# First stage of a hybrid decoder kernel: latents leave PSUM on ScalarE, norm reciprocals in token columns, weights split two chunks ahead, a gate chunk moved

## The chip, the cores and the metric

The kernel runs on one core of a Trainium2 chip. The metric is the device time of one launch in microseconds (us), the median of three runs. The engines are called as in the profile: PE (TensorE; PEld is its weight load), DVE (VectorE), ACT (ScalarE), POOL (GpSimd) and SP (SyncE, which here only issues DMAs).

## The reference, cut to what matters

A decoder trunk over 2048 tokens of width 1024: two branches on one normed input, recurrence (RWKV-7) and latent attention, merged by gates, then a mixture of experts. The change is in the first part alone, which projects the input and prepares both branches:

```python
h = rmsnorm(x, mix_norm_g[l])
cols = h @ w_in[l]
c_rw  = cols[..., :RW_COLS]                       # recurrence: r, k, v and three small inputs
c_q   = cols[..., RW_COLS:RW_COLS + Q_LORA]       # 384 query latents
c_kv  = cols[..., ...:... + KV_LORA]              # 256 key-value latents
c_kr  = cols[..., ...:RW_COLS + MLA_COLS]         # 32 rotary key columns
gate_rw  = jax.nn.sigmoid(cols[..., ...])         # 1024
gate_mla = jax.nn.sigmoid(cols[..., ...])         # 1024
y_rw  = rwkv7_mix(c_rw, ...)
# in mla_mix:
q  = (rmsnorm(q_d,  g_qa)  @ w_q_up)
kv = (rmsnorm(kv_d, g_kva) @ w_kv_up)

def rmsnorm(x, g):
    y = x * lax.rsqrt(jnp.mean(x * x, axis=-1, keepdims=True) + NORM_EPS)
    return y * g
```

## The kernel before

Everything is held transposed, columns of the projection in partitions and tokens along the free axis. `phase_a` goes through two halves of 1024 tokens, each as two blocks (n = 0, 1) of 512. The projection's columns are cut into chunks of 128. For one chunk and one block `a_mm` runs 24 products 128x128x512 (`mm3`: weights and input are each split into a high and a low part in the fast f32 format, and three of the four products are kept), into one of the four PSUM banks tagged `am`. All other products of the stage use four banks tagged `rw`.

Weights: `a_weights` loads a chunk (512 KB) into one of two `awr` buffers. `a_split` makes the two parts of it, `aw0` and `aw1`, two buffers each: a copy on ACT (L143), then a subtraction (L144), on DVE for the first part of a half and on POOL for the later one. `a_mm` keeps two chunks split (`len(self.live) < 2`). `worder` is the order of the chunks: 14 of the recurrence, five gate chunks, two of key-value latents, three of query latents, one gate chunk, the rotary key, ten gate chunks.

The input's norm is not applied to the input. `x_squares` adds squares of the raw input (ACT, then POOL), and `x_rms` turns the sums over partitions into `xrs`, the factor of each token, repeated over all 128 partitions: one product with a matrix of ones (`sums`, L214), a square root on ACT, a reciprocal on DVE, both over 128x512. Each evicted block is multiplied by `xrs` on its way out of PSUM: `cols` for the recurrence, `gate` (L633, then a tanh on ACT and a store), and `mla_evac` (L259) for the latents, which also squares them (ACT, L261) and adds the squares up in `zacc` (DVE, L263). Latents wait in `zc`, two buffers. `mla_norm` then makes a second factor `zrs` for the latents in the same way with `sums`, multiplies and splits them (L283); `mla_up` multiplies them with the up-projections.

The recurrence units (`rw_unit`, eight in each half) prepare each pair of heads: decays, keys, `f` (the factor on the key and then the key itself, L521 and L522), the masked score products `aa` (L551, L554), and at the end three transposes that go through the tile `tok` (L592, one buffer) to DRAM by four stores each.

`invert` is a triangular inverse on DVE, 124 small operations that run behind everything else from the key-value chunks to the end of the half.

Generators in a list (`gens`) are advanced by `bg(k)` after each block; the order in which the program writes instructions is a priority. What each engine really executes, and in which order, is planned when the kernel is built: a list scheduler with a timeline simulation takes, on each engine, the ready instruction with the highest priority, and hands out the buffers. The result is a fixed order for each engine, and the engine waits wherever the chip is later than the plan.

Of the kernel before, what the change touches and what calls it, by code (L numbers as in the profile page):

```python
# [44 lines left out]
BIG = 1 << 20  # L45

CST = {}
CFIRST = 128


def _consts():
# [36 lines left out]
class K:  # L88
# [67 lines left out]
    def rope_tables(self, pool):  # L156
# [3 lines left out]
        self.ropeT = self.dram("ropeT", [2, 8, 16, S])  # L160
        pi = pool.tile(sh, I32, name="posi")
        self.dma(pi, self.I["pos"])
        a, n, z, s, c, u = (pool.tile(sh, F32, name="rt_" + k) for k in "anzscu")
        nc.gpsimd.tensor_copy(u, pi)
        nc.gpsimd.tensor_scalar(a, u, self.c["invp"], None, op0=OP.mult)
        ts = lambda o, i, s1, s2, o1, o2: nc.gpsimd.tensor_scalar(o, i, s1, s2, op0=o1, op1=o2)
# [40 lines left out]
            self.dma(xs[:, k], self.I["xT"][k, :, c0:c0 + 512])  # L207
        return xs

    def sums(self, acc, n, scale):  # L210

        nc = self.nc
        ps = self.pst("rw", 4)
        nc.tensor.matmul(ps, self.c["ones"], acc, start=True, stop=True)  # L214
        nc.scalar.activation(n, ps, AF.Sqrt, scale=scale, bias=self.eps[:, 0:1])
        nc.vector.reciprocal(n, n)

    def x_squares(self, pool, xs, n):
        nc = self.nc
# [6 lines left out]
            yield  # L226

    def x_rms(self, n):
        self.rs[n] = self.ap.tile([128, 512], F32, name="xrs%d" % n)
        self.sums(self.xacc[n], self.rs[n], 1.0 / D)  # L230

    def h_make(self, xs, n, k):

# [19 lines left out]
    def mla_evac(self, pool, ps, key, n, j):  # L253
        nc = self.nc
        if j == 0:
            self.zc[key, n] = (pool.tile([128, 3, 512], F32, name="zc", bufs=2),
                               pool.tile([128, 512], F32, name="zacc", bufs=2))
        zc, acc = self.zc[key, n]
        nc.vector.tensor_tensor(out=zc[:, j], in0=ps, in1=self.rs[n], op=OP.mult)  # L259
        sq = pool.tile([128, 512], F32, name="zsq") if j else acc  # L260
        nc.scalar.activation(sq, zc[:, j], AF.Square)  # L261
        if j:
            nc.vector.tensor_tensor(out=acc, in0=acc, in1=sq, op=OP.add)  # L263
# [9 lines left out]
    def mla_norm(self, pool, key, n):  # L273
        nc = self.nc
        zc, acc = self.zc.pop((key, n))
        nk, g0, dim = (3, 50, 384) if key == "q" else (2, 53, 256)
        yield "w"
        yield "w"
        rt = pool.tile([128, 512], F32, name="zrs")
        self.sums(acc, rt, 1.0 / dim)  # L280
        cT = [pool.tile([128, 3, 512], F32R, name="cT%d" % j, bufs=2) for j in range(2)]
        for k in range(nk):
            nc.vector.scalar_tensor_tensor(zc[:, k], zc[:, k], self.pv[:, g0 + k:g0 + k + 1], rt,  # L283
                                           op0=OP.mult, op1=OP.mult)
            self.split(cT[0][:, k], cT[1][:, k], zc[:, k])
        self.cT[n] = cT
# [136 lines left out]

    def a_split(self):
        rv = self.wraw.pop(0)
        hl = [self.ap.tile([128, 8, 128], F32R, name="aw%d" % j, bufs=2) for j in range(2)]
        if rv.shape[2] == 64:

            hl = [hl[0][:, :, :64], hl[0][:, :, 64:], hl[0]]
        self.split(hl[0], hl[1], rv, self.nc.gpsimd if self.wsplit > 1 and self.wsplit % 35 > 18 else None)  # L430
        self.live.append((self.worder[self.wsplit], hl))
        self.wsplit += 1
        self.a_weights()

    def a_mm(self, ci, n, last):
        while len(self.live) < 2 and self.wraw:
            self.a_split()
        w = dict(self.live)[ci]
        ht = self.ht[n]
# [23 lines left out]
    def rw_unit(self, pool, p, q, zr, zk, zv, x1, xg):  # L463
# [117 lines left out]
        for j, src in enumerate(("b", "k", "v")):  # L581
# [6 lines left out]
            ps = self.pst("rw", 4)  # L588
            for i in range(4):
                nc.tensor.transpose(ps[:, i * 128:(i + 1) * 128], x[:, i * 128:(i + 1) * 128], self.ident)  # L590
            tk = t("tok")
            A.activation(tk, ps, AF.Copy)  # L592
            tv = tk.rearrange("p (c h d) -> p c h d", c=4, h=2)
            for e in range(2):
# [5 lines left out]
    def phase_a(self):  # L600
# [3 lines left out]
        with ExitStack() as st:  # L604
# [2 lines left out]
            ap = self.ap = st.enter_context(pool("acols"))  # L607
            self.rw_setup()
            self.mla_setup()
            self.worder = 2 * (tuple(range(14)) + G[:5] + KV + Q + G[5:6] + ("kr",) + G[6:])  # L610
            self.wpos = self.wsplit = 0
            self.wraw, self.live, self.ht, self.zc, self.rs, self.cT, self.xacc = [], [], [[None] * 8, [None] * 8], {}, {}, {}, {}
            gens = []

            def bg(k):
# [42 lines left out]
            xp = start.enter_context(pool("start"))  # L658
            self.consts()
            xs = [self.x_load(xp, 0, 0, True)]  # L660
            self.dma(self.c["ones"], self.I["cst"][:, :CFIRST])
            xs.append(self.x_load(xp, 0, 1))
            for n in range(2):
                gens.append(self.x_squares(xp, xs[n], n))
# [4 lines left out]
            for half in range(2):  # L669
# [46 lines left out]
                with pool("mla%d" % half) as mp:  # L716
# [7 lines left out]
                            bg(3)  # L724
                    next(inv)
                    gens.append(self.mla_up(mp, "kv", half))
                    for j, ci in enumerate(Q):
                        for n in range(2):
                            self.mla_evac(mp, self.a_mm(ci, n, n == 1), "q", n, j)
                            if j == 2:  # L730
                                gens.append(self.mla_norm(mp, "q", n))
                            bg(3)
                            next(inv, None)
                    gens.append(self.mla_up(mp, "q", half))
                    for ci in G[5:6] + ("kr",) + G[6:6]:
                        for n in range(2):
                            if ci == "kr":
                                self.kr_evac(mp, self.a_mm("kr", n, n == 1), half * 1024 + n * 512, n)
                            else:
                                gate(ci, n, half)  # L740
                            bg(3)
                            next(inv, None)
                    drain()
                with pool("gates%d" % half) as gp:
                    if half == 0:
# [1066 lines left out]
```

## Time and profile before

| | us |
|---|---|
| three runs | 2708.5, 2710.17, 2712.07 |
| median | 2710.17 |
| profiled execution | 2706.18 |
| its span, first to last instruction | 2704.4 |

The profiled execution is one more run, with the hardware profiler on. Its trace tells for each instruction when it ran, how long the engine was idle before it, and which semaphore ended that wait. A busy share is a mean over stages; what a change in a stage is worth is read from the waits in that stage. The granted clock is the share of TensorE's full clock that the chip allows at a time.

### The profile page before, as it was taken

What the parts mean: (1) busy time and instruction counts of PE and PEld (TensorE: products, weight loads), DVE (VectorE), ACT (ScalarE), POOL (GpSimd) and SP (SyncE); (2) the same over time, 40 slices, a digit from 0 to 9 for tenths busy, and PEclk for the clock granted to TensorE, in tenths of its full rate; (3) what the DMA queues carried; (4) which work ended last, traced back from release to release, by engine and by line L of the source; (5) the groups of instructions that cost most, each with busy time, mean ns of one, the idle gap of its engine ahead of it and who ended that gap; (6) DMA issues with size and microseconds to landing.
All of it is one profiled execution on the core that took longest, in us unless ns stands there. A gap on an engine that the chain in (4) does not pass through costs nothing. (4 is left out here: it accounts for less than half of the span.)

```text
span 2704.4 us, 42459 instructions
## 1 busy us (share of the span) xinstructions
PE 2493.0 (92%) x14868; PEld 2033.2 (75%) x14868; DVE 1957.0 (72%) x3466; ACT 1424.3 (53%) x2539; POOL 961.8 (36%) x676
## 2 busy tenths in 40 slices
PE   8999999999999998989999999999999878999991
PEld 6777778788787886767777777777888667989880
DVE  8766699777748994676666766666666678888883
ACT  6554243465443423666776767632232246878774
POOL 3111612401112222556665665402012145555540
PEclk9999999999999998999999999999999979999995
DMA  4556444435563435444443441674554377999987
GB/s 147 125 146 172 137 140 134 171 102 133 142 177 105 138 122 173 129 122 133 129 123 95 129 129 41 205 225 137 184 167 148 125 228 235 329 288 318 299 246 264
DMA packets 334443, 452.46 MB, mean 167 GB/s; under 512 B 170320, under 2 KB 216272, under 8 KB 332944
## 3 DMA queue, kind: packets, MB, share of 16 engines
q1 hardware_dynamic: 320656, 416.03, 49.3%
q0 software_dynamic: 13568, 33.67, 5.5%
q8 instruction: 118, 1.93, 0.3%
q14 instruction: 101, 0.83, 0.1%
HBM read 318.06 MB, written 138.33 MB: 169 GB/s over the span
## 5 line engine op out<-in xcount | busy, mean ns | idle before, releaser
L151 PE MATMUL am<-h,aw 128*128 128x512 f32 x1104 | 440.8, 400 | 21.2 <-ACT h L237 8.5
L144 POOL TENSOR_TENSOR pl<-pf,ph 128x512 fp32r<-128x512 f32 (+1 forms) x320 | 372.8, 1181 | 238.5 <-ACT ph L143 163.3
L153 PE MATMUL am<-h,aw 128*128 128x512 f32 x1104 | 437.8, 397 | 11.9 <-POOL aw L144 7.5
L152 PE MATMUL am<-h,aw 128*128 128x512 f32 x1104 | 437.3, 396 | 0.1
L1562 PE MATMUL gg<-hh,gu 128*128 128x256 f32 (+5 forms) x1024 | 271.0, 338 | 5.4 <-DVE hh L144 5.0
L151 PEld LDWEIGHTS am<-h,aw 128*128 128x128 f32 x1104 | 210.8, 191 | 70.1 <-ACT h L237 8.5
L153 PEld LDWEIGHTS am<-h,aw 128*128 128x128 f32 x1104 | 210.3, 191 | 60.3 <-POOL aw L144 8.7
L1563 PE MATMUL gg<-hh,gu 128*128 128x128 f32 (+5 forms) x1024 | 249.2, 250 | 0.0
L152 PEld LDWEIGHTS am<-h,aw 128*128 128x128 f32 x1104 | 210.5, 191 | 48.6 <-DVE h L238 2.4
L1052 ACT ACTIVATE pf<-st 128x512 f32<-128x512 f32 (+1 forms) x320 | 167.6, 529 | 119.2 <-PE st L1046 65.2
L1562 PEld LDWEIGHTS gg<-hh,gu 128*128 128x128 f32 x1024 | 195.8, 191 | 13.1 <-DVE hh L144 6.6
L1563 PEld LDWEIGHTS gg<-hh,gu 128*128 128x128 f32 x1024 | 198.6, 194 | 4.5
L143 ACT ACTIVATE ph<-pf 128x512 fp32r<-128x512 f32 (+1 forms) x320 | 176.8, 565 | 6.6
L985 DVE TENSOR_REDUCE mx<-sh 128x1 f32<-128x512 f32 x192 | 128.2, 686 | 66.1 <-PE sh L982 64.9
L144 POOL TENSOR_TENSOR aw<-awr,aw 128x1024 fp32r<-128x1024 f32 (+1 forms) x32 | 89.0, 2782 | 241.2 <-ACT aw L143 231.0
L144 DVE TENSOR_TENSOR gu<-graw,gu 128x1024 fp32r<-128x1024 f32 x128 | 155.0, 1239 | 12.0 <-ACT gu L143 10.3
L143 ACT ACTIVATE gu<-graw 128x1024 fp32r<-128x1024 f32 x128 | 131.1, 1056 | 33.8 <-DMA graw<-in_moe_w_gu 31.4
L801 DVE TENSOR_TENSOR inv<-inv,invt 128x62 f32<-128x62 f32 (+30 forms) x124 | 137.9, 1112 | 2.8
L144 POOL TENSOR_TENSOR sum<-sq,sum 128x512 fp32r<-128x512 f32 x16 | 23.5, 1469 | 317.1 <-ACT sum L143 301.3
L799 DVE TENSOR_TENSOR invt<-inv 128x62 f32<-128x62 f32 (+30 forms) x124 | 133.5, 1076 | 2.6
L1044 PE MATMUL st<-aq,ak 97*128 97x512 f32 (+1 forms) x320 | 127.5, 398 | 8.0 <-ACT pf L1052 7.1
L1580 POOL DMA_INDIRECT x2d<-yo,ix x50 | 93.0, 1860 | 104.2 <-DMA x2d<-yo,ix 21.5
(414 smaller groups left out, 6342.8 us busy)
## 6 DMA issues: line engine op xcount, KB each, us to landing
graw<-in_moe_w_gu SPq DMA_DIRECT2D x128, 512.0 KB
awr<-in_w_cols SPq DMA_DIRECT2D x70, 512.0 KB
draw<-in_moe_w_down SPq DMA_DIRECT2D x62, 512.0 KB
gate<-gsb SPq DMA_DIRECT2D x64, 256.0 KB
SC<-SCd SPq DMA_DIRECT2D x32, 512.0 KB
wbr<-in_w_b SPq DMA_DIRECT2D x32, 512.0 KB
gt<-gate SPq DMA_DIRECT2D x32, 512.0 KB
xs<-in_xT SPq DMA_DIRECT2D x32, 256.0 KB
```

What stands on the lines that cost most here:

```text
L143: nc.scalar.activation(hi, src, AF.Copy)
L144: (eng or nc.vector).tensor_tensor(out=lo, in0=src, in1=hi.bitcast(F32), op=OP.subtract)
L151: nc.tensor.matmul(ps, lh, rh, start=first and i == 0, stop=False)
L152: nc.tensor.matmul(ps, lh, rl, start=False, stop=False)
L153: nc.tensor.matmul(ps, ll, rh, start=False, stop=last and i == n - 1)
L799: V.tensor_tensor(out=tv, in0=m[:, 0:t, t:t + 1].to_broadcast([128, t, n]), in1=m[:, t:t + 1, t + 1:].to_broadcast([128, t, n]), op=OP.mult)
L801: V.tensor_tensor(out=m[:, 0:t, t + 1:], in0=m[:, 0:t, t + 1:], in1=tv, op=OP.add)
L985: V.reduce_max(mx[:, j, kb:kb + 1], ps[:, :n], axis=AX)
L1044: T.matmul(ps[:, cs], kk[0][:, ks], qq[0][:, cs], start=True, stop=False)
L1052: A.activation(pf[:, cs], ps[:, cs], AF.Exp, scale=SCALE)
L1562: T.matmul(*a, start=k == 0, stop=False)
L1563: T.matmul(*b, start=False, stop=k == 7)
```

## The change

- `mla_evac`: the latents leave PSUM by a copy on ACT, without the factor `xrs`; squares and sums are those of the raw latents.
- `sums`: four products with the accumulated squares as the loaded operand and one column of ones as the other. The sums come out with a token in each partition, 128x4 for a block of 512.
- `x_rms` and `mla_norm`: root and reciprocal are taken on 128x4. `mla_norm` first multiplies the sums twice by the input's factor and the result once more, so that one factor holds both norms. `spread` brings a 128x4 factor back to 128x512: a broadcast copy on DVE into a buffer of `xacc`, and four products with the identity. `x_rms` copies the result out of PSUM on ACT; `mla_norm` uses it in PSUM.
- `CFIRST`: the identity comes with the first 256 columns of the constants, ahead of the second input block.
- `a_split`, `a_mm`: three buffers for the split weights, three chunks kept split.
- The sixth gate chunk stands between the key-value and the query chunks.
- Buffers: `tok` shares the one buffer of `f`; four of the six work tiles of `rope_tables` are taken from two `r1` buffers; `zrs` (128x512) is gone.

```diff
-CFIRST = 128
+CFIRST = 256
@@ rope_tables
-        a, n, z, s, c, u = (pool.tile(sh, F32, name="rt_" + k) for k in "anzscu")
+        a, s = (pool.tile(sh, F32, name="rt_" + k) for k in "as")
+        n, z, c, u = (t[:, o:o + 256] for t in [pool.tile([128, 512], F32, name="r1", bufs=2) for _ in range(2)]
+                      for o in (0, 256))
@@
-    def sums(self, acc, n, scale):
-        nc = self.nc
+    def sums(self, acc):
         ps = self.pst("rw", 4)
-        nc.tensor.matmul(ps, self.c["ones"], acc, start=True, stop=True)
-        nc.scalar.activation(n, ps, AF.Sqrt, scale=scale, bias=self.eps[:, 0:1])
-        nc.vector.reciprocal(n, n)
+        for i in range(4):
+            self.nc.tensor.matmul(ps[:, i:i + 1], acc[:, i * 128:(i + 1) * 128], self.c["ones"][:, 0:1],
+                                  start=True, stop=True)
+        return ps[:, :4]
+
+    def spread(self, col):
+        b = self.ap.tile([128, 512], F32, name="xacc", bufs=2).rearrange("p (i c) -> p i c", i=4)
+        self.nc.vector.tensor_copy(b, col[:, :, None].to_broadcast([128, 4, 128]))
+        ps = self.pst("rw", 4)
+        for i in range(4):
+            self.nc.tensor.matmul(ps[:, i * 128:(i + 1) * 128], b[:, i], self.ident, start=True, stop=True)
+        return ps
@@ x_rms
-        self.sums(self.xacc[n], self.rs[n], 1.0 / D)
+        rc = self.rc[n] = self.ap.tile([128, 4], F32, name="xrc%d" % n)
+        nc.scalar.activation(rc, self.sums(self.xacc[n]), AF.Sqrt, scale=1.0 / D, bias=self.eps[:, 0:1])
+        nc.vector.reciprocal(rc, rc)
+        nc.scalar.activation(self.rs[n], self.spread(rc), AF.Copy)
@@ mla_evac
-        nc.vector.tensor_tensor(out=zc[:, j], in0=ps, in1=self.rs[n], op=OP.mult)
+        nc.scalar.activation(zc[:, j], ps, AF.Copy)
@@ mla_norm
-        rt = pool.tile([128, 512], F32, name="zrs")
-        self.sums(acc, rt, 1.0 / dim)
+        rt, rc, sums = pool.tile([128, 4], F32, name="zrt", bufs=2), self.rc[n], self.sums(acc)
+        for x in (sums, rt):
+            nc.vector.tensor_tensor(out=rt, in0=x, in1=rc, op=OP.mult)
+        nc.scalar.activation(rt, rt, AF.Sqrt, scale=1.0 / dim, bias=self.eps[:, 0:1])
+        nc.vector.reciprocal(rt, rt)
+        nc.vector.tensor_tensor(out=rt, in0=rt, in1=rc, op=OP.mult)
+        rt = self.spread(rt)
@@ a_split
-        hl = [self.ap.tile([128, 8, 128], F32R, name="aw%d" % j, bufs=2) for j in range(2)]
+        hl = [self.ap.tile([128, 8, 128], F32R, name="aw%d" % j, bufs=3) for j in range(2)]
@@ a_mm
-        while len(self.live) < 2 and self.wraw:
+        while len(self.live) < 3 and self.wraw:
@@ rw_unit
-            tk = t("tok")
+            tk = t("tok", tag="f")
@@ phase_a
-            self.worder = 2 * (tuple(range(14)) + G[:5] + KV + Q + G[5:6] + ("kr",) + G[6:])
+            self.worder = 2 * (tuple(range(14)) + G[:5] + KV + G[5:6] + Q + ("kr",) + G[6:])
...
-            self.dma(self.c["ones"], self.I["cst"][:, :CFIRST])
+            self.dma(self.cst[:, :CFIRST], self.I["cst"][:, :CFIRST])
...
                     gens.append(self.mla_up(mp, "kv", half))
+                    for n in range(2):
+                        gate(G[5], n, half)
+                        bg(3)
+                        next(inv, None)
                     for j, ci in enumerate(Q):
...
                     gens.append(self.mla_up(mp, "q", half))
-                    for ci in G[5:6] + ("kr",) + G[6:6]:
-                        for n in range(2):
-                            if ci == "kr":
-                                self.kr_evac(mp, self.a_mm("kr", n, n == 1), half * 1024 + n * 512, n)
-                            else:
-                                gate(ci, n, half)
-                            bg(3)
-                            next(inv, None)
+                    for n in range(2):
+                        self.kr_evac(mp, self.a_mm("kr", n, n == 1), half * 1024 + n * 512, n)
+                        bg(3)
+                        next(inv, None)
```

## Rows read from the trace of the kernel before

**Rows 1.** The page, its first part: for each engine busy us, share of the span and number of instructions (PEld is TensorE's weight load).

```profile
PE 2493.0 (92%) x14868; PEld 2033.2 (75%) x14868; DVE 1957.0 (72%) x3466; ACT 1424.3 (53%) x2539; POOL 961.8 (36%) x676
```

**Rows 2.** Busy time by stretches of the first stage: from:to and length in us, then busy us (and number of instructions) of PE, PEld, DVE, ACT and POOL, the granted TensorE clock, the DMA engines' mean busy share and GB/s. The last line is the whole stage.

```profile
290.00:350.00 60.00, 50.95 (x199) 39.47 (x198) 52.07 (x57) 15.22 (x24) 45.05 (x42) 0.91 0.35 116
...
350.00:486.00 136.00, 135.39 (x639) 113.02 (x638) 132.11 (x133) 49.24 (x86) 35.06 (x16) 1.00 0.49 160
...
486.00:515.00 29.00, 22.36 (x79) 17.23 (x78) 24.54 (x25) 10.58 (x17) 21.36 (x13) 0.82 0.29 110
...
1026.00:1056.00 30.00, 22.22 (x81) 16.63 (x80) 12.82 (x10) 12.11 (x14) 10.99 (x4) 0.83 0.55 137
...
0.00:1056.00 1056.00, 1002.24 (x4810) 812.01 (x4811) 807.47 (x991) 453.74 (x794) 239.28 (x146) 0.98 0.49 141
```

**Rows 3.** The waits of PE from 0 to 1056 us: who waited for whom, us in total, times, longest.

```profile
PE rw L567 <- DVE aa L554: 12.9, 8, 2.4
```

**Rows 4.** The timeline of PE, only instructions ahead of which PE stood idle: start us, duration us, engine, line, operation, tiles, form, count, and in brackets the idle time before it with what ended it.

```profile
39.60 0.47 PE L151 MATMUL am<-h,aw 128*128 128x512 f32 x1 [2.37 <-DVE ex L494]
...
308.47 0.50 PE L153 MATMUL am<-h,aw 128*128 128x512 f32 x1 [1.35 <-POOL aw L144]
...
315.31 1.12 PE L214 MATMUL rw<-zacc,cst 128*128 128x512 f32 x2 [1.56 <-DVE zacc L263]
...
325.10 2.01 PE L214 MATMUL rw<-zacc,cst 128*128 128x512 f32 x2 [3.07 <-DVE zacc L263]
...
343.19 0.80 PE L151 MATMUL am<-h,aw 128*128 128x512 f32 x1 [3.08 <-DVE zc L259]
...
493.79 0.80 PE L153 MATMUL am<-h,aw 128*128 128x512 f32 x1 [3.73 <-POOL aw L144]
...
509.87 0.80 PE L153 MATMUL am<-h,aw 128*128 128x512 f32 x1 [2.37 <-POOL aw L144]
...
861.34 0.80 PE L151 MATMUL am<-h,aw 128*128 128x512 f32 x1 [2.97 <-DVE zc L259]
...
1038.15 0.50 PE L151 MATMUL am<-h,aw 128*128 128x512 f32 x1 [3.19 <-ACT aw L143]
...
1043.91 0.79 PE L153 MATMUL am<-h,aw 128*128 128x512 f32 x1 [3.54 <-DVE aw L144]
```

**Rows 5.** The six stretches up to 1056 us in which the granted clock was below 1: from:to and length, busy us of PE (and its instructions), granted clock, DMA share and GB/s.

```profile
325.14:328.55 3.41, 3.41 (x6) 0.50 0.00 0
...
342.21:349.04 6.83, 5.86 (x14) 0.50 0.25 88
...
492.39:499.22 6.83, 5.43 (x13) 0.50 0.22 52
...
509.46:512.87 3.41, 3.00 (x7) 0.50 0.73 308
...
861.03:864.44 3.41, 3.10 (x7) 0.50 0.00 0
...
1038.53:1048.77 10.24, 6.70 (x17) 0.50 0.42 93
```

**Rows 6.** Groups of instructions up to 1056 us: line, engine, operation, tiles, form, count, busy us in all, mean ns of one, and the engine's idle time just before them with its causes.

```profile
L216 DVE RECIPROCAL zrs<-zrs 128x512 f32<-128x512 f32 x8 | 26.7, 3342 | 0.4 <-ACT zrs L215 0.4
...
L259 DVE TENSOR_TENSOR zc<-am,xrs 128x512 f32<-128x512 f32 x20 | 13.2, 673 | 0.0
...
L308 ACT ACTIVATE uo<-rw 128x512 f32<-128x512 f32 x32 | 18.0, 585 | 2.2 <-PE rw L153 1.1 <-ACT aw L143 0.6 <-ACT uo L308 0.4
...
L994 DVE TENSOR_SCALAR mr<-m 128x4 fp32r<-128x4 f32 x6 | 1.7, 288 | 0.2
```

**Rows 7.** Small products on PE: from the timeline eight products of one unit's transposes (128x128 loaded for each) and sixteen 64-column records of the recurrence, and the group of weight loads of the sums of squares (columns as in rows 6).

```profile
137.00 1.04 PE L590 MATMUL rw<-cst,hat 128*128 128x128 f32 x8
...
1090.23 0.69 PE L880 MATMUL sx<-SV,SC 128*64 128x64 f32 x16
...
L214 PEld LDWEIGHTS rw<-zacc,cst 128*128 128x128 f32 x16 | 3.0, 202 | 6.7 <-issue 4.4 <-DVE zacc L263 2.0
```

**Rows 8.** The timeline of ACT around the first square root of the key-value norms.

```profile
322.30 0.63 ACT L261 ACTIVATE zsq<-zc 128x512 f32<-128x512 f32 x1 [7.08 <-DVE zc L259]
...
322.95 1.28 ACT L215 ACT_TABLE_LOAD   x1
```

**Rows 9.** The timeline of POOL at the end of the first half.

```profile
490.98 2.76 POOL L144 TENSOR_TENSOR aw<-awr,aw 128x1024 fp32r<-128x1024 f32 x1
```

**Rows 10.** The timelines of ACT and of the DMA queue SP (SPq: issue times) in the recurrence units, sorted by start: the tile `f` of two units, first and third `tok` of the first one, the first `tok` of the next, and the issues of the stores of the second and third `tok`.

```profile
121.61 0.82 ACT L521 ACTIVATE f<-ta,halfvec 128x512 f32<-128x512 f32 x1
...
138.28 0.59 ACT L592 ACTIVATE tok<-rw 128x512 f32<-128x512 f32 x1
...
147.91 0.80 ACT L521 ACTIVATE f<-ta,halfvec 128x512 f32<-128x512 f32 x1
...
148.04 2.56 SPq L96 DMA_DIRECT2D BKd<-tok  x4
...
152.25 0.60 ACT L592 ACTIVATE tok<-rw 128x512 f32<-128x512 f32 x1 [0.87 <-DMA BKd<-tok]
...
153.38 2.58 SPq L96 DMA_DIRECT2D Vd<-tok  x4
...
163.49 0.59 ACT L592 ACTIVATE tok<-rw 128x512 f32<-128x512 f32 x1
```

More of the change, by code (lines that the diff above doesn't have):

```diff
@@ L228, in x_rms @@
     def x_rms(self, n):
+        nc = self.nc
         self.rs[n] = self.ap.tile([128, 512], F32, name="xrs%d" % n)
-        self.sums(self.xacc[n], self.rs[n], 1.0 / D)
+        rc = self.rc[n] = self.ap.tile([128, 4], F32, name="xrc%d" % n)
+        nc.scalar.activation(rc, self.sums(self.xacc[n]), AF.Sqrt, scale=1.0 / D, bias=self.eps[:, 0:1])
+        nc.vector.reciprocal(rc, rc)
+        nc.scalar.activation(self.rs[n], self.spread(rc), AF.Copy)
     def h_make(self, xs, n, k):
@@ L609, in phase_a @@
             self.mla_setup()
-            self.worder = 2 * (tuple(range(14)) + G[:5] + KV + Q + G[5:6] + ("kr",) + G[6:])
+            self.worder = 2 * (tuple(range(14)) + G[:5] + KV + G[5:6] + Q + ("kr",) + G[6:])
             self.wpos = self.wsplit = 0
-            self.wraw, self.live, self.ht, self.zc, self.rs, self.cT, self.xacc = [], [], [[None] * 8, [None] * 8], {}, {}, {}, {}
+            self.wraw, self.live, self.ht, self.zc, self.rs, self.rc, self.cT, self.xacc = [], [], [[None] * 8, [None] * 8], {}, {}, {}, {}, {}
             gens = []
```

## Prediction

> **What bounds the kernel now.** The page comes first: TensorE (PE) is busy for 92% of the span, more than any other engine [rows 1]. That is a mean over stages, so the second view is a table of stretches [rows 2]. The first stage, which the change is about, ends near 1056 us. PE is busy 1002.2 of those, so it stands idle for 54. The idle time is not spread evenly: 290 to 350, 486 to 515 and 1026 to 1056 lose 9.0, 6.6 and 7.8 us, while 350 to 486 loses 0.6 with VectorE (DVE) busy 132.1 of 136. So this stage is bound by PE, and only what PE waits for, or what is added to PE, can move the end. The largest wait by total is not one of the three stretches: 12.9 us, eight times, for the masked score products of the recurrence units [rows 3].
>
> The PE timeline says what ended each long wait [rows 4]: at the start 2.37 us; then between key-value and query chunks 1.35 for split weights, 1.56 and 3.07 for the sums of squares, 3.08 for the raw latents' way out of PSUM; at the end of the first half 3.73 and 2.37 for weights split on GpSimd; in the second half 2.97 for the latents and 3.19 and 3.54 for split weights. Behind each of the longer ones the granted clock stands at 0.50, the 1.2 of the two levels 1.2 and 2.4 GHz [rows 5]. Half of PE's busy time in such a stretch is lost as well: 1.7, 2.9, 2.7, 1.5, 1.6 and 3.4 us.
>
> **The change part by part.**
>
> *Latents by ScalarE, reciprocals in token columns.* DVE loses twenty evictions of 673 ns (13.2 us) and twelve wide reciprocals of 3.34 us (40.1) [rows 6]. It gains twelve broadcast copies; the nearest 128x512 row of DVE is the eviction's, so 8.1 us, and about forty operations on 128x4, nearest 288 ns, so 11.5. DVE is relieved by some 34 us, of which only what PE waited for counts. ScalarE (ACT) gains twenty evictions of 585 ns [rows 6]; it is far from full in every stretch of [rows 2], so that is taken at nothing (cover gone: 11.7).
>
> *On PE.* The product with ones streams 512 columns of f32. The new spread streams the same 512 in four pieces, so it replaces that one. The four column sums come on top: eight f32 records (the trace has two per f32 product), each a 128x128 load and one column. No row shows one. From below, sixteen small records take 0.69 us, so eight take 0.34; from above, the sums' own weight load, 202 ns, so 1.6; nearest in form are eight products with a 128x128 load of their own in 1.04 us, with more columns [rows 7]. I take 0.8. Twelve norms: 9.6 us, ends 4.1 and 19.4, all on the engine that sets the end. For this price alone the Trainium skill (TensorE: Matmul & The Clock Gate, section LDWEIGHTS) has a formula of columns over 1.2, thus 107 ns per load, an estimate of 0.85 per norm and 10.2 for twelve; no run here shows that product.
>
> Each norm of the latents now leaves PE and returns to it twice instead of once. PE takes its instructions in a fixed order, so a late spread stops it as the late sums did. Those waits were 1.56, 3.07 and, in the six other latent norms, none. Eight spreads at 0.5 are 4 us; ends 0 and 18 (eight at their mean).
>
> A tanh gate chunk now runs among the square roots of the key-value norms, and a table load costs ACT 1.28 us [rows 8]. Four more in each half are 10 us of an engine that has the room, in a chain whose 3.34 us reciprocal has gone: nothing (from outside: 10). The Trainium skill (ScalarE: Activation LUTs, section What ACT_TABLE_LOAD costs) adds a drain of 1.38 us to each, which speaks against this edit; by it the eight would be 21 us of ACT. The timeline does not show it in front of the load at 322.95: the square before it ends at 322.93 [rows 8].
>
> *A gate chunk between.* Query latents need the two `zc` buffers that the key-value norms still hold; four blocks fill the four `am` banks and PE stops. Two gate blocks in between give the norms two blocks' time and need no `zc`. I count 3.08 and 2.9 of clock in the first half, 2.97 and 1.6 in the second: 10.5. Of the two waits for the sums (6.3 with the clock) I count half, 3.2, since the add that is late stays on DVE behind the inverse, and PE's order still meets it; ends 0 and 6.3.
>
> *Weights two chunks ahead.* The split of the chunk after next no longer needs PE to finish the present one first, only a raw buffer that has landed. At 490.98 the subtraction stood on GpSimd among the squares' adds of the next half [rows 9]; issued a chunk earlier, it stands ahead of them. I count 1.35, then 3.73 and 2.37 with 4.2 of clock: 11.6. In the last stretch (10.1 with the clock) the same engines split attention's first operands, so I count three quarters, 7.6; ends 0 and 10.1. Splits, their DMAs and the engines of each keep their number.
>
> *Start.* 64 KB more ahead of the second input block is 0.4 us of transfer even at the 160 GB/s of a quiet stretch [rows 2], beside PE's first block: nothing (uncovered: 0.4). Of the 2.37 wait behind DVE I count 1.5. The angle tables borrow `r1` buffers that the query up-projection uses only at its end, behind the whole key-value part: nothing; without that cover it would wait for a table's store.
>
> *`tok` moves into the buffer of `f`.* This is the part that adds a wait. A unit's `f` must now wait until the three `tok` of the unit before have left by DMA; ACT stands in order behind it, DVE's `f` product behind that, then the scores and PE. Read from [rows 10]: `tok` at 138.28, the third at 152.25, its four issues end at 155.96, and the 1.65 us that the earlier store took after its last issue (150.60 to 152.25) puts the buffer free at 157.6, 19.3 after the first. From `f` to the unit's next `tok` it is 15.6 (147.91 to 163.49). One turn of the buffer is then 34.9 us, against 26.3 from `f` to `f` today. But of the 15.6 only about 8 must follow `f` (its own 0.8, two products, the scores and their masks, the bonus); the other 7.6 is work that can run while `f` waits. That leaves 27.3, an excess of 1.0 over fourteen handovers, 14 us. Most of it is hidden by ten gate blocks that need no unit; I take 4, ends 0 and 136 (9.7 at each of fourteen, nothing hidden).
>
> **Sum.** Gains 10.5 + 3.2 + 11.6 + 7.6 + 1.5 = 34.4. Costs 9.6 + 4 + 4 = 17.6. The profiled execution took 2706.2 us, with a span of 2704.4: 2706.2 - 16.8 = 2689.4. The median of the three runs is 4.0 above it, so 2693. A difference of 0.2%, 5.4 us, is about what can be told here from none.
>
> **The rivals.**
>
> *The shared buffer stretches the units (slower).* Place: `f` in each recurrence unit. Price: 14 us for each microsecond that a handover gains and PE cannot fill. It decides from 1.2 us (16.8 over fourteen). For it: the turn of 34.9 as the rows stand, and the 12.9 us for which PE already waits for units. Against it: ACT waits for the bonus store in each turn today, so a turn already has room to be packed. At 3 us the gain of 20.8 without this term becomes a loss of 21.2: 2731.
>
> *Added PE work and spread waits eat the gain (no change).* At their upper ends, 19.4 and 18, they meet the 34.4: 2713. For it: PE is the bound. Against it: three quarters of the latent norms waited for nothing.
>
> *Everything counted goes, and the units' waits with it.* All listed waits with their clock are 40.9 us, 12.9 more for the scores, less 4.1: 49.7, so 2660. For it: 34 us of DVE relief. Against it: the scores are late behind work that the change does not lighten.
>
> **How the numbers follow.** The forecast has 0.52, the stretched units 0.26, no change 0.12, everything 0.10. The forecast's own range, from its terms' nearer ends, is 2674 to 2704. For 8 in 10 the range reaches most of the way to the third rival, 2664, and to the stretched units at 3 us, 2735; left out are larger stretches and the rest of the best case. Faster by over 0.2%: 0.62; within: 0.12; slower: 0.26.
>
> **What would show it.** Right: the two waits for `zc` gone, the sums at about 0.8 us, the wide reciprocals gone from the DVE groups, no wait of PE for `aw` near the end of either half, and `f` following `f` at about 26 us. Wrong: `f` waiting for a `tok` store, with units 29 us or more apart and PE waiting for `aa`; or PE idle in front of the spread with the clock at 0.50 after it. What would make the forecast wrong above all is the order of instructions, which is planned anew for the whole stage.

## The result, and the profile after

| | median us | lowest to highest | runs |
|---|---|---|---|
| kernel before | 2709.34 | 2700.38 to 2712.07 | 4 |
| changed kernel | 2743.08 | 2738.07 to 2752.11 | 4 |

The ratio is 1.0128, with a 95% interval of 1.0104 to 1.0153. The change makes the kernel slower by 34 us. The forecast was 2693, in a range that ends at 2735: the sign is wrong, and the time lies above the range. The profiled execution of the changed kernel took 2752.11 us.

First PE's waits in the first stage of the changed kernel (who waited for whom: us in total, times, longest), then the stage and two stretches of it with their columns as in [rows 2], and last the stage of the kernel before up to its own end:

```profile
PE am L151 <- ACT zc L275: 27.1, 2, 14.4
PE rw L572 <- DVE bk L544: 13.1, 4, 6.2
PE rw L226 <- DVE xacc L223: 11.5, 6, 5.6
PE am L151 <- ACT h L252: 8.2, 1, 8.2
PE rw L588 <- DVE aa L575: 5.8, 5, 1.6
PE am L153 <- DVE aw L144: 4.1, 1, 4.1
```

```profile
0.00:1110.50 1110.50, 1030.10 (x5006) 837.03 (x5006) 777.79 (x1015) 472.06 (x825) 239.72 (x146) 0.97 0.48 135
290.00:350.00 60.00, 46.19 (x226) 37.08 (x224) 23.29 (x30) 20.85 (x33) 25.87 (x23) 0.89 0.50 135
350.00:486.00 136.00, 124.91 (x597) 103.91 (x598) 131.89 (x158) 52.36 (x92) 40.94 (x29) 0.96 0.40 130
```

```profile
0.00:1061.90 1061.90, 1008.14 (x4837) 816.93 (x4838) 810.39 (x1002) 454.37 (x795) 242.11 (x146) 0.98 0.49 141
```

The last product of the projections starts at 1110.5 us, against 1061.9 before: 49 us late. PE is busy 22 us longer up to there and idle 27 us longer (80.4 against 53.8). The stretch that lost 0.6 us of PE before [rows 2] now loses 11.1. The wait for `zc` that the change was to take away [rows 4] has become the largest of all, ended by ScalarE instead of VectorE. The waits for `aw` did go, but for one.

What ScalarE does in this time is in its timeline: two `f` with the `tok` ahead of the first, and then the end of the last unit of the half (start, duration, form, and in brackets the idle time before it):

```profile
88.59 0.58 ACT L613 ACTIVATE tok<-rw 128x512 f32<-128x512 f32 x1
...
104.17 0.58 ACT L613 ACTIVATE tok<-rw 128x512 f32<-128x512 f32 x1
...
109.29 0.82 ACT L542 ACTIVATE f<-ta,halfvec 128x512 f32<-128x512 f32 x1 [1.69 <-DMA Vd<-tok]
...
120.82 0.60 ACT L613 ACTIVATE tok<-rw 128x512 f32<-128x512 f32 x1
...
137.42 0.60 ACT L613 ACTIVATE tok<-rw 128x512 f32<-128x512 f32 x1 [1.84 <-DMA BKd<-tok]
142.80 0.81 ACT L542 ACTIVATE f<-ta,halfvec 128x512 f32<-128x512 f32 x1 [3.93 <-DMA Vd<-tok]
...
322.63 0.60 ACT L613 ACTIVATE tok<-rw 128x512 f32<-128x512 f32 x1 [6.01 <-DMA BKd<-tok]
327.52 0.60 ACT L613 ACTIVATE tok<-rw 128x512 f32<-128x512 f32 x1 [4.29 <-DMA BKd<-tok]
328.02 2.06 ACT L275 ACTIVATE zc<-am 128x512 f32<-128x512 f32 x4
```

Seven of the eight `f` of the first half wait for a store of `tok`, 20.4 us in all. From one `f` to the next it is 33.9 us in the first half and 33.0 in the second (means of seven), against 27.0 and 29.8 before. The last three lines are the other end of it: the last unit's `tok` come so late that they meet the key-value chunks. ScalarE stands in order in front of them for 6.01 and 4.29 us, and four evictions of latents, which VectorE did before, stand behind. PE, whose next product needed one of the four `am` banks, waited 12.66 us there (from 316.0 to 328.66) and 14.45 at the same place of the second half.

### The profile page after: what moved, and what is told of

Same layout as the page of the kernel before. It is cut to its first block, busy times and chain, and to the rows that moved or that the text cites. A ratio compares the mean times of both kernels' runs of the same rounds, so it can differ in the third digit from the quotient of the medians.

```text
span 2750.3 us, 42822 instructions
## 1 busy us (share of the span) xinstructions
PE 2517.7 (92%) x15036; PEld 2055.0 (75%) x15036; DVE 1928.7 (70%) x3482; ACT 1441.3 (52%) x2569; POOL 961.2 (35%) x676
## 4 chain that ended last, share of the span: by engine, by line
PE 46%; DVE 21%; DMA 11%; issue 10%; ACT 6%; SPq 4%; POOL 0%; DVEq 0%; ACTq 0%; POOLq 0%
SPq L96 4%; DVE invt L821 3%; PE am L151 3%; PE am L152 3%; PE am L153 3%; PE gg L1584 3%; DVE inv L823 3%; PE st L1066 3%; PE sh L1004 2%; PE pv L1058 2%; PE pv L1053 2%; PE st L1067 2%; PE st L1068 2%; PE pv L1054 2%; DVE gu L144 2%
## 5 line engine op out<-in xcount | busy, mean ns | idle before, releaser
L151 PE MATMUL am<-h,aw 128*128 128x512 f32 x1104 | 440.1, 399 | 35.3 <-ACT zc L275 27.1
L1584 PEld LDWEIGHTS gg<-hh,gu 128*128 128x128 f32 x1024 | 194.7, 190 | 13.1 <-DVE hh L144 4.9
L143 ACT ACTIVATE gu<-graw 128x1024 fp32r<-128x1024 f32 x128 | 130.7, 1055 | 27.1 <-DMA graw<-in_moe_w_gu 26.6
L821 DVE TENSOR_TENSOR invt<-inv 128x62 f32<-128x62 f32 (+30 forms) x124 | 126.7, 1021 | 2.5
L823 DVE TENSOR_TENSOR inv<-inv,invt 128x62 f32<-128x62 f32 (+30 forms) x124 | 124.3, 1002 | 2.4
```

What stands on the lines that cost most here:

```text
L143: nc.scalar.activation(hi, src, AF.Copy)
L151: nc.tensor.matmul(ps, lh, rh, start=first and i == 0, stop=False)
L821: V.tensor_tensor(out=tv, in0=m[:, 0:t, t:t + 1].to_broadcast([128, t, n]), in1=m[:, t:t + 1, t + 1:].to_broadcast([128, t, n]), op=OP.mult)
L823: V.tensor_tensor(out=m[:, 0:t, t + 1:], in0=m[:, 0:t, t + 1:], in1=tv, op=OP.add)
L1584: T.matmul(*a, start=k == 0, stop=False)
```

## The experiments

Ratios are to the kernel before on the same chip, with their 95% interval. "Stage end" is the start of the last projection product in the profiled execution; before it is 1061.9.

**Is it the shared buffer?**

```diff
# e1_own_tok: the changed kernel with
-            tk = t("tok", tag="f")
+            tk = t("tok", tag="zwa")
# e2_before_tok_in_f: the kernel before with
-            tk = t("tok")
+            tk = t("tok", tag="f")
# e7_before_tok_in_zwa: the kernel before with
-            tk = t("tok")
+            tk = t("tok", tag="zwa")
```

> The changed kernel with one edit: `tok` takes the buffer of `zwa`, which is free once the units run, instead of that of `f`. Theory S (the shared buffer stretches the units): units return to about 26 us from `u` to `u` (32.6 in the changed kernel), the two waits for `zc` on ACT (12.7 and 14.5) go, and the time falls below the kernel before, to the forecast without that term, about 2689 (2675 to 2702). Theory N (the norms' second trip through PE or the eviction by ACT is the cause): units may quicken, but the time stays within 10 of 2743.

> The kernel before with one edit: `tok` takes the buffer of `f`. Theory S: units at 31 to 34 us, the stage longer by 35 to 65, so 2745 to 2775. Theory N: within 10 of the kernel before, 2700 to 2720.

> The kernel before with one edit: tok shares the buffer of zwa. It says whether e1_own_tok and e4_before_three_aw carry a cost from that buffer. If the sharing is free, as taken so far: within 4 us of before and f following f at about 27 us. If not: units 29 us or more apart and 2720 or more, and both must be read anew.

Measured: e1 2718.91 us, ratio 1.0031 (1.0017 to 1.0044), stage end 1072.6. e2 2748.78, ratio 1.0147 (1.0118 to 1.0176), stage end 1092.3. e7 2715.39, ratio 1.0001 (0.9986 to 1.0016): the buffer of `zwa` is free of charge. The shared buffer alone costs some 40 us on the kernel before, and taking it out of the changed kernel gives most of the 34 us back: 24 by the medians, 26 by the ratios. In e1 `f` follows `f` at 27.0 and 26.3 us, in e2 at 34.3 and 35.5; in e2, seven `f` waited for a store of `tok`, 22.2 us in the first half. In e1 PE waits no more for `zc`:

```profile
PE rw L226 <- DVE xacc L223: 13.4, 4, 6.2
PE rw L588 <- DVE aa L575: 12.8, 10, 2.7
PE am L151 <- ACT h L252: 8.3, 1, 8.3
PE rw L151 <- ACT uo L329: 4.0, 1, 4.0
```

```profile
0.00:1072.60 1072.60, 1029.43 (x5005) 837.07 (x5006) 759.05 (x1018) 470.50 (x825) 236.26 (x146) 0.98 0.49 140
```

The second fence is the stage up to its end: PE is busy 21 us longer than in the 1061.9 us before, and idle for 43.2 us instead of 53.8. Against the 80.4 of the changed kernel, 37 us of idle time have gone. So the shared buffer's cost is shown. But e1 is not the 21 us faster than before that the rest of the sum had promised; it is 8 slower.

**What are the gate chunk and the three split chunks worth?**

```diff
# e3_before_gate_between: the kernel before with the gate chunk moved, as in the change
# e4_before_three_aw: the kernel before with
-        hl = [self.ap.tile([128, 8, 128], F32R, name="aw%d" % j, bufs=2) for j in range(2)]
+        hl = [self.ap.tile([128, 8, 128], F32R, name="aw%d" % j, bufs=3) for j in range(2)]
-        while len(self.live) < 2 and self.wraw:
+        while len(self.live) < 3 and self.wraw:
#   (for room: tok in zwa, rope tables in r1 and rb)
# e6_gate_and_three_aw, e13_gate_aw3_again: both together
# e8_changed_gate_at_old_place: e1 with the gate chunk where it was
```

> The kernel before with the gate chunk moved between key-value and query chunks, nothing else. If the gate blocks cover the `zc` buffers, the waits of 3.08 and 2.97 and the low clock behind them go: 5 to 11 us faster, about 2701. The rival, that the wait only moves to the sums of squares or elsewhere: within 4 of the kernel before.

> The kernel before with weights split two chunks ahead (three `aw` buffers), and what makes room for them: `tok` in the buffer of `zwa`, the angle tables in `r1` and `rb`. If the splits were late for want of a buffer, the waits for `aw` at the end of both halves go: 12 to 22 us faster, about 2692. The rival, that ACT and GpSimd are late by their other work: within 5 of the kernel before.

> The kernel before with the gate chunk between key-value and query chunks and three split chunks together (tok shares the buffer of zwa and the rope tables that of r1, for room); norms and latents as before. Theory A (each edit only hands its wait to the next): the two effects seen alone, 0 and -6, add up: about 2706, and PE still waits some 10 us in all between 290 and 400 and at the ends of the halves. Theory B (each was held back by the other's wait: with the gate alone PE waited for split weights, with three chunks alone for zc): both sets of waits go, 2690 to 2698. If B holds, the rest of the change (norms and latents) costs e1_own_tok some 20 to 28 us.

> The changed kernel with tok in the buffer of zwa, as e1_own_tok, and the sixth gate chunk back behind the query chunks. Theory A (the gate chunk's place is worth nothing by itself): 2715 to 2722, as e1_own_tok. Theory B (it is worth what was counted once split weights and latents no longer stand in the way): PE waits for zc again, some 6 us with 4 of clock in the two halves, 2726 to 2732.

Measured: e3 2712.74, ratio 0.9998 (0.9982 to 1.0014). e4 2704.30, ratio 0.9978 (0.9960 to 0.9997). e6 2702.11, ratio 0.9953 (0.9937 to 0.9969), and once more as e13 (below) 0.9964 (0.9950 to 0.9978). e8 2721.75, ratio 1.0026 (1.0014 to 1.0038), within its error where e1 stands. e4 and e6 are faster than both kernels, e6 by more. The place of the gate chunk is worth nothing measurable by itself on either kernel; three split chunks are worth some 6 us, both together 10 to 13, with intervals that overlap that of e4. PE's waits in e3, and then in e6, say why it is not the 29.7 us that the prediction counted for the two:

```profile
...
PE rw L151 <- ACT cT L143: 7.5, 3, 3.3
...
PE rw L151 <- ACT uo L348: 3.2, 2, 2.4
```

```profile
...
PE am L153 <- DVE aw L144: 4.9, 3, 3.6
PE rw L151 <- ACT cT L143: 4.6, 3, 2.7
PE rw L216 <- DVE zacc L265: 3.5, 2, 2.9
PE rw L151 <- ACT uo L350: 3.4, 2, 1.7
PE am L151 <- DVE gsb L635: 3.2, 1, 3.2
```

```profile
0.00:1056.90 1056.90, 1007.20 (x4837) 816.89 (x4838) 811.03 (x997) 459.94 (x799) 242.89 (x146) 0.99 0.49 142
```

In e3 the 6.0 us for `zc` are gone, and 7.5 for the split latents `cT` have come. In e6 PE stands idle for 49.7 us up to the stage's end (1056.90 less 1007.20, the last fence), before for 53.8: a listed wait that goes leaves VectorE or ScalarE late at the next place.

**What do the norms and the latents cost?**

```diff
# e5_norms_alone: the kernel before with sums, spread, x_rms of the change, the identity first, and in mla_norm
+        nc.scalar.activation(rt, self.sums(acc), AF.Sqrt, scale=1.0 / dim, bias=self.eps[:, 0:1])
+        nc.vector.reciprocal(rt, rt)
+        rt = self.spread(rt)
# e9_changed_latents_by_dve: e1 with mla_norm as in e5 and
-        nc.scalar.activation(zc[:, j], ps, AF.Copy)
+        nc.vector.tensor_tensor(out=zc[:, j], in0=ps, in1=self.rs[n], op=OP.mult)
# e10_norms_and_latents: e5 with mla_evac and mla_norm of the change
```

> The kernel before with the norms' part of the change alone: sums as four one-column products, roots and reciprocals on 128x4, broadcast copy and four products with the identity, and the identity loaded with the first constants. Latents leave by VectorE with the factor, two split chunks, gate chunk and tok as before. Theory P (the products are what it costs): in e1_own_tok a norm's sums took 0.81 us of PE and its spread 0.81 to 0.92 at the full clock, against 0.46 for the wide product, so 1.2 more for each of twelve, 14 us, and up to the 11 us of spread waits seen there, less the 4.6 us for which PE waits for the sums before: 2725 to 2735. Theory D (VectorE's relief of some 34 us pays for it): the same as before or faster, 2695 to 2712.

> The changed kernel with tok in the buffer of zwa (e1_own_tok), and the latents leaving PSUM on VectorE with the input's factor, as before; so the three small multiplications per latent norm go too. Norms in token columns, gate chunk between and three split chunks stay. It is e6_gate_and_three_aw (-11) plus the norms of e5_norms_alone (0), and e1_own_tok (+8) less the latents' part. Theory L (the latents' part costs the 20 us between those sums: three more VectorE steps in each norm's chain, behind the inverse, before the spread): 2698 to 2706. Theory N (the norms' 17 us of PE work was hidden in e5_norms_alone by waits that the gate chunk and the split chunks take away, so it shows here): 2716 to 2722, as e1_own_tok.

> e5_norms_alone plus the latents' part: raw latents leave by ScalarE, and the latent norms multiply by the input's factor on 128x4. Gate chunk, two split chunks and tok as before. Theory L: about 20 us over e5_norms_alone, 2728 to 2735, with longer PE waits for the spread's broadcast copy than the 12.0 us there. Theory N: as e5_norms_alone, 2709 to 2716.

Measured: e5 2712.51, ratio 1.0000 (0.9986 to 1.0014), stage end 1066.7. e9 2715.60, ratio 1.0020 (1.0009 to 1.0030), stage end 1069.2. e10 2708.34, ratio 1.0004 (0.9991 to 1.0017). The latents' way out is worth nothing measurable (e10 against e5, e1 against e9). The norms cost nothing on the kernel before, where theory P (the products are the cost) had put 2725 to 2735, but some 15 to 18 us on top of e6. In e5 PE waits 12.0 us for the spread's copy, in three, and in return the waits for `zc` (6.0 before), most of those for `zacc` (4.6) and 4.4 us of those for `aa` are gone. On e6 there is less left to trade. The stage of e9 up to its end, beside that of e6 above:

```profile
0.00:1069.20 1069.20, 1023.63 (x5005) 832.20 (x5006) 770.58 (x1014) 458.30 (x805) 234.15 (x146) 0.99 0.49 140
```

PE is busy 16.4 us longer than in e6, as in e5 against before (1024.5 and 1008.1), but its idle time falls only from 49.7 to 45.6, where in e5 it fell from 53.8 to 42.2. So up to the stage's end e9 is later by PE's busy time, part of it at the low clock, and not by more idle time.

**What makes the spread late, and is it the products?** First e1's timeline of PE at the first norm of the latents, with a spread and the next sums at the full clock at the end, and then VectorE's:

```profile
318.00 1.80 PE L216 MATMUL rw<-cst,zacc 128*128 128x1 f32 x8 [1.91 <-DVE zacc L279]
...
337.78 2.05 PE L226 MATMUL rw<-cst,xacc 128*128 128x128 f32 x8 [6.25 <-DVE xacc L223]
...
426.06 1.05 PE L226 MATMUL rw<-cst,xacc 128*128 128x128 f32 x8
426.94 0.95 PE L216 MATMUL rw<-cst,zacc 128*128 128x1 f32 x8
```

```profile
330.60 0.91 DVE L821 TENSOR_TENSOR invt<-inv 128x650 f32<-128x650 f32 x1
331.44 0.68 DVE L654 TENSOR_TENSOR gsb<-am,xrs 128x512 f32<-128x512 f32 x1
332.04 0.14 DVE L297 TENSOR_TENSOR zrt<-rw,xrc 128x4 f32<-128x4 f32 x1
332.11 0.82 DVE L823 TENSOR_TENSOR inv<-inv,invt 128x650 f32<-128x650 f32 x1
332.85 0.35 DVE L297 TENSOR_TENSOR zrt<-zrt,xrc 128x4 f32<-128x4 f32 x1
...
337.02 0.62 DVE L223 COPY xacc<-zrt 128x512 f32<-128x512 f32 x1
```

The sums leave PE before 320; VectorE reads them first at 332.04 (0.14 us), with eight operations of the inverse, one add of squares and one gate block in between, and it is busy all the time. The copy comes 17 us after the sums. The test leaves the inverse out (its two operations on `m` in each step):

> e1_own_tok without the 124 small VectorE operations of the triangular inverse (that part of the computation is left out, so its time is not to be set against the others'; what counts is PE's wait in front of the spread). If these operations, between which the norm's six small VectorE steps stand in order, are what makes the spread late: the waits for the broadcast copy, 13.4 us in four (6.25 and 4.75 the longest), shrink to under 3 us in all, and the clock stays at 1.00 between 330 and 350 us. If the chain's own length through two engines makes it late: they stay above 8 us.

```profile
318.10 0.16 DVE L297 TENSOR_TENSOR zrt<-rw,xrc 128x4 f32<-128x4 f32 x1
318.30 0.16 DVE L297 TENSOR_TENSOR zrt<-zrt,xrc 128x4 f32<-128x4 f32 x1
320.31 0.18 DVE L299 RECIPROCAL zrt<-zrt 128x4 f32<-128x4 f32 x1 [1.85 <-ACT zrt L298]
320.53 1.92 DVE L300 TENSOR_TENSOR zrt<-zrt,xrc 128x4 f32<-128x4 f32 x1
322.48 0.59 DVE L223 COPY xacc<-zrt 128x512 f32<-128x512 f32 x1
```

Measured, by VectorE's timeline above: from the first multiplication to the copy 4.4 us. PE's waits for the copy are 0.2 us in all, the clock stays at 1.00 from 221 us to the stage's end, and that comes at 1038.6 instead of 1072.6. (The whole took 3048.03 us, on other data from there on, and is not compared.) So the inverse's operations on VectorE make the spread late. Whether it is their place in the order or the amount of their work this run cannot tell, since it takes both away. The products were then tried without the waits:

```diff
# e12_six_products_each_norm: e6 with
         ps = self.pst("rw", 4)
+        for i in range(6):
+            nc.tensor.matmul(ps[:, i:i + 1], acc[:, i % 4 * 128:(i % 4 + 1) * 128], self.c["ones"][:, 0:1],
+                             start=True, stop=True)
         nc.tensor.matmul(ps, self.c["ones"], acc, start=True, stop=True)
```

> The kernel of e6_gate_and_three_aw with six one-column products (128x128 loaded for each, 12 records) into the norm's PSUM tile ahead of each of the twelve wide products, which then overwrites them. That is the amount of PE work by which a norm in token columns exceeds a wide one, at e1's 0.81 us for eight records: 1.2 us each, 14.6 us for twelve. No step is added on VectorE or ScalarE, and no wait. Theory N1 (products alone are what the norms cost here): 13 to 17 us over e13_gate_aw3_again, so about 2715, where e9_changed_latents_by_dve stands. Theory N2 (it is the waits of PE in front of the spread, 12.4 us in e9): within 4 us of e13_gate_aw3_again. In between: both, in that proportion.

> The kernel of e6_gate_and_three_aw once more, as the base for e12 on the same chip, and because it is the only version so far that beats both kernels: 2698 to 2706, a ratio of 0.994 to 0.997 to the kernel before. A ratio of 0.999 or more would say that its gain was not one.

Measured on one chip: e12 2704.88, ratio 0.9966 (0.9952 to 0.9981); e13 2707.07, ratio 0.9964 (0.9950 to 0.9978). The products are there, 1.25 us for each norm, and the stage ends later in the profile, at 1064.4 against 1055.3 in e13 and 1056.9 in e6:

```profile
0.00:1064.40 1064.40, 1019.00 (x4982) 830.66 (x4982) 806.59 (x1001) 456.15 (x797) 239.62 (x146) 0.99 0.49 141
```

Yet the whole is no slower. By the whole's time theory N1 (the products alone are the cost) falls, although up to the stage's end e12 looks like e9 (PE busy 1019.0 us, idle 45.4). Last, the inverse was kept and its steps written later:

```diff
# e14_e9_inverse_held_back, e15_e6_inverse_held_back: e9 and e6 without next(inv, None) in the two gate
# blocks and the first four query blocks, and in the gate blocks behind
                         elif i < 16:
                             next(inv, None)
+                            if i < 6:
+                                next(inv, None)
```

> The kernel of e9_changed_latents_by_dve with six steps of the inverse moved: none is written in the two gate blocks and the first four query blocks, and two instead of one in the first six gate blocks behind. The amount of work is the same. Theory N2 (the norms cost what PE waits in front of the spread, since the norm's small VectorE steps stand in order among the inverse's): those waits, 12.4 us in six in e9 and most of them at the key-value norms, fall to 6 or less with the low clock around 330 us, and the time falls by 5 to 10 us against e9, to about the kernel before or below. Rival: the wait only moves to what the inverse is late for at the end of each half, and the time stays within 3 us of e9 (ratio 1.001 to 1.003).

> The same move of the inverse's steps in the kernel of e6_gate_and_three_aw, whose norms are wide: the control for e14. Theory N2: little to gain, since only 3.5 to 4.2 us of PE's waits there are for the sums' squares behind the inverse: a ratio of 0.993 to 0.997 to the kernel before, as e6 and e13. If it gains as much as e14 does against e9, the place of the inverse is what costs, with either kind of norm.

Measured: e14 2718.05, ratio 1.0033 (1.0018 to 1.0049), e15 2706.45, ratio 0.9977 (0.9955 to 0.9998). Nothing is gained: e14 stands within the error of e9, e15 within that of e6 and a little above the ratio expected. In e14 PE's wait is almost that of e9 (12.3 us in five, 7.4 the longest):

```profile
PE rw L226 <- DVE xacc L223: 11.0, 5, 7.5
```

The edit did not remove what it was to remove: from 290 to 350 us VectorE executes the same instructions in the same order in both, so none of the moved steps had stood ahead of the first key-value norm, where the longest wait is. e14 therefore does not tell what that wait costs; the time stayed about where the rival had it, but nothing shows that a wait moved.

**What stays open.** e9 is 15 to 18 us slower than e6; their stage ends differ by 12.3, and e12, whose stage ends 7.5 after e6's, is not slower at all. e4's stage ends 12.0 us earlier than before, but its time is only 6 us shorter; e2's ends 30 us later, and its time is 40 us longer. In the profiled executions the stretch from the last projection product to the first product into the experts' bank `gt` (L1466 before) took from 1084.0 us (e10) to 1109.3 (e7), 1096.1 before, and the order of its instructions was planned anew for each kernel. Differences of the stage under some 10 us therefore don't show one for one in the time, and what the norms' waits cost in the time, apart from their products, was not isolated.

## Why the prediction was wrong

**The step that failed: `tok` in the buffer of `f`, taken at 4 us.** It is the rival "The shared buffer stretches the units", held at 0.26, in its mechanism; the term measured 24 to 26 us of the time (e1 against the changed kernel), not 4. The turn of the buffer was read from the rows as 15.6 + 14.0 + 5.3 = 34.9 us, and then cut to 27.3, because 7.6 of the 15.6 were "work that can run while `f` waits". The changed kernel's turn is 11.5 from `f` to the first `tok` (109.29 to 120.82), 16.6 to the third (137.42) and 5.4 to the next `f` (142.80): 33.5. So 4.1 of the 7.6 could be packed, and 2.6 came back in the middle, where ScalarE, in order, also waits for the bonus store ahead of `kraw`: 5.84 us in this unit, 4.21 in the turn that the prediction read. The 1.65 us from a store's last issue to `f` held to the hundredth: the issues of the third `tok` end at 107.64, `f` starts at 109.29. The uncut 34.9 was nearly right.

The rival's example was 3 us for each handover (from one unit's `f` to the next) that PE cannot fill. Against e1 the handovers gained 6.9 and 6.7 us, 95 us over fourteen, and the stage ended 37.9 us later: 2.7 us for each handover were not filled. What PE did in the other 57 is not shown in detail.

**The parts against the sum.** e6, e9, e1 and the changed kernel form a chain, each with one more part of the change. By their ratios (0.9953, 1.0020, 1.0031, 1.0128) the gate chunk and three split chunks gain 13 us, the norms cost 18 (10 and 15 by e13), the latents by ScalarE 3 and the shared buffer 26, each to some 4 us. The sum had a gain of 29.7, a cost of 8.9 for the norms (9.6 and 4, less the 3.2 and 1.5 counted at the sums and the start), nothing and 4. The misses are 17, 9, 3 and 22 us: the buffer is the largest, the gains are the second.

**What was missed:** the two edits to ScalarE meet. Its twenty evictions were costed at nothing, since it is not full in any stretch [rows 2], and the cover was priced at their busy time, 11.7 us. But they stand in order behind the late `tok`: 27.1 us of PE's waits in two places. This says where PE waited, not that the evictions cost that much. In e2 the latents leave by VectorE, and there it is their squares on ScalarE (L261) that stand behind the same late `tok`, and PE waits 19.0 us for the sums:

```profile
322.84 0.60 ACT L592 ACTIVATE tok<-rw 128x512 f32<-128x512 f32 x1 [8.12 <-DMA BKd<-tok]
327.67 0.60 ACT L592 ACTIVATE tok<-rw 128x512 f32<-128x512 f32 x1 [4.23 <-DMA BKd<-tok]
328.16 1.14 ACT L261 ACTIVATE zacc<-zc 128x512 f32<-128x512 f32 x2
```

```profile
PE rw L214 <- DVE zacc L263: 19.0, 2, 10.1
```

**Added PE work, 9.6 us: the column sums right at the full clock, the spread wrong.** A norm's column sums take 0.81 us from their start to the next product's at the full clock, as taken (0.8). But the spread takes 0.88 (426.06 to 426.94), where the prediction had it replace the wide product, 0.46: pieces of 128 columns with a load each are not the price of 512 columns. From start to start, without the waits, the sums of e1 hold PE for 12.2 us (three of them at the low clock) and the spreads for 12.4, the wide products before for 7.8: 16.8 more. The estimate of 0.85 per norm from the Trainium skill (TensorE: Matmul & The Clock Gate, section LDWEIGHTS) agrees with the measured 0.81 of the column sums; applied to the eight loads of the spread too, it would have given it nearly what it took. That added PE work moves the end was the first premise of the sum, and e12 bore it out for the stage's end, but not for the whole.

**Waits before the spread, 4 us:** 11.5 us in six in the changed kernel, 13.4 in four in e1, inside the stated 0 to 18 but in its upper half. The prediction counted them by the two sums that had waited before. It did not go through the steps between sums and spread, five on VectorE and a root on ScalarE (the text before e11 counts six on VectorE), of which the five stand in order among the inverse's operations. The waits are followed by the low clock, in e1 behind that of 6.25 us:

```profile
335.16:345.40 10.24, 7.62 (x27) 6.74 (x28) 10.14 (x12) 2.59 (x6) 5.61 (x4) 0.50 0.54 185
```

**Gains, 34.4 us:** 10 to 13 measured for gate chunk and three split chunks (e6, e13), against 29.7 for those two lines. In e6 the listed waits went for the most part (those for split weights from 16.1 to 4.9 us, those for `zc` from 6.0 to none), and others came near the same places. That VectorE's relief is not a gain by itself was right (e5, e10). A tanh chunk among the roots cost nothing that e3 or e8 shows.

**Slips in the sums that do not move the forecast.** "It decides from 1.2 us" divides 16.8 by fourteen, but 16.8 already holds the term's own 4; 20.8 gives 1.5. The upper end of 136 (9.7 at each handover) is not the difference of the 34.9 and 26.3 beside it, which is 8.6 and gives 120. And 26.3 is one pair of units; the means before are 27.0 and 29.8.

**Signs named beforehand:** `f` waiting for a `tok` store and units 29 us or more apart were seen. PE waiting for `aa` was not: that wait fell from 12.9 to 5.8 us, since the units wait one step earlier, for `bk` (13.1 us), which needs `f`. The low clock behind a late spread was seen too.

## What to carry to other kernels

When a single buffer is shared by a tile that leaves by DMA and a tile that starts the next unit, add up the whole turn, with the store's issues and landing, and forecast with that sum; work that "can run meanwhile" runs only as far as the fixed order of the waiting engine lets it. An engine with much idle time can still be late for an instruction that PE needs: ask what the instruction ahead of that one waits for. And a wait that ends last can be worth less than its length and its clock: here, of 29.7 us listed, 10 to 13 came back.

## What had not been expected of the hardware

On PE, four f32 products with one column and a 128x128 load each took 0.81 us and four with 128 columns 0.80 to 0.92, both at the full clock: here it hardly mattered whether a product had one column or 128. Six more such products in each of twelve norms, 15 us of PE time from start to start, left the kernel's time as it was (2704.88 against 2707.07 us on the same chip), although the stage ended 9 us later in the profile.
